# One-token shift of the values: each 127-row transfer made as one of 112 rows and one of 15 rows

## The chip, the cores and the metric

The kernel runs on one core of a Trainium2 chip. The core has a matrix engine (TensorE, PE in the profile), a vector engine (VectorE, DVE), a scalar engine (ScalarE, ACT), a general engine (GpSimd, POOL) and a sync engine (SyncE, SP), which issues nearly all DMA transfers here. Each engine works through its own instructions in order, and they wait for one another through semaphores. 16 DMA engines carry out the transfers. The metric is the device time of one execution in microseconds (us).

## The reference

One layer of a decoder trunk for 1024 tokens of width 1024, all in float32. After an RMSNorm, one projection gives q, k and v (8 heads of 64) and two inputs of a gated convolution branch. The two branches are joined, projected, added to x, and a feed-forward part of width 2816 with a short convolution follows.

```python
h = rms_norm(x, norm1_g)
q, k, v, glu_a, glu_b = split(h @ w_in)
A = stick_breaking_attention(rms_norm(q), rms_norm(k), v)
c = causal_depthwise_conv(glu_a * sigmoid(glu_b))     # 31 taps, 512 channels
C = silu(layer_norm(c))
x = x + concat([A, C]) @ w_out
gate, val = split(rms_norm(x, norm2_g) @ w_up)
x = x + (silu(causal_depthwise_conv(gate)) * val) @ w_down
```

The attention's weights are `beta[t,s] * prod_{s<j<t} (1 - beta[t,j])`, with `beta = sigmoid(q.k / 8)` and s < t. Such a weight is the difference of two neighbouring running products. So the kernel can leave the running products as they are and multiply them by differences of neighbouring values, `v[s-1] - v[s]`. For that it needs v shifted by one token.

## The kernel before, in words

Tokens lie on the 128 partitions (rows), in 8 tiles of 128 tokens. Float32 products are made in three matmuls from a high and a low part of each operand (`mm3`, lines 318 to 321): ACT copies the high part, DVE or GpSimd subtracts to get the low part. The weights of the first stage are loaded and split in this way by `weights` (load L461, high part L465, low part L469).

The heads are worked in two blocks of four. `project` makes q, k and v for a block; v of a block is `[128, 8, 256]`: row, token tile, four heads' values. The functions that matter here, in the order of the work:

- `glu` makes one of four channel blocks of the convolution. TensorE multiplies for both halves of the tokens; ACT evicts the gate (L627) and DVE the product (L629) into `cpad`. Then DVE runs 16 and 15 taps (`conv_a` L650, L652; `conv_b` L660, L662), while ACT (L669, L676) and GpSimd (L679) build the rest of the sum, which DVE joins (L692 to L694).
- `differences` (L479) shifts v of one block by one token into `ahead` (L492, L493), and GpSimd then subtracts (L501), in two halves of four token tiles. It is called for block 0 early, among the convolutions, and for block 1 when the last products of the first stage are done.
- `conv_norm` normalizes the convolution's output in two token halves: TensorE transposes (L715, L741), DVE takes statistics (L719, L720) and normalizes (L723), ACT applies the gate (L745, L768) and copies a high part (L763), DVE or GpSimd make the low part (L774), and SP stores both to device memory (`conv_d`, L785). The high and low parts lie in four rooms, the `nb` rooms, which the first convolution used before and the attention uses after; one of them already holds the first head's keys at that time.
- The attention then goes through the heads: transposes of keys (`kT`, L1054) and queries (`qT`, L1088), scores (`z`, L1131, L1132), sigmoid (L1139), a running product by a scan (L1153), its transpose (`wT`, L1180) and the product with the differences (`po`, L1208). `qk` products of the second block (`queries_keys_in`) run beside it.

After that come the output projections, the feed-forward's up products (`u`, 22 steps) and down products (`dn`, L1807).

What sets the order is a planner, `Plan`. Each operation is added with a cost for each engine that may do it, a due time (`key`) and what it must come after. `run` then chooses greedily, one operation at a time, by the earliest possible start and the due time, and `in_order` fixes the resulting order for PE, DVE, ACT and GpSimd. SP isn't fixed by it: the order of the transfers on SP is left to the framework's scheduler, which also moved other loads between the two halves of one shift. For SP the planner has a model of its own (lines 180 to 184): `kb` is the size of an operation's transfers and `dmas` their number.

```python
for _ in range(op.dmas):
    at[e] = max(at[e] + 60, landed[-8] if len(landed) > 7 else 0)
    dma = max(dma, at[e] + (2300 if start < 3000 else 1300)) + op.kb * 2.6 / op.dmas
    landed.append(dma + 600)
op.end = landed[-1]
```

Of the kernel before, what the change touches and what calls it, by code (L numbers as in the profile page):

```python
# [16 lines left out]
P = 128  # L17
# [39 lines left out]
class Plan:  # L57
# [32 lines left out]
    def add(self, cost, *args):  # L90
        if not isinstance(cost, dict):
            cost, args = {cost: args[0]}, (lambda eng, f=args[1]: f(),) + args[2:]
        op = Plan.Op()
        op.shares = "DVE2" in cost
        op.cost, op.emit, op.key = {e.rstrip("2"): c for e, c in cost.items()}, args[0], args[1]
        op.after = list(args[2]) if len(args) > 2 else []
        op.takes = list(args[3]) if len(args) > 3 else []
        op.end, op.engine, op.n, op.kb, op.dmas = None, None, len(self.ops), 512, 1
        self.ops.append(op)
        return op  # L100
# [101 lines left out]
def kernel(  # L202
# [21 lines left out]
    nc = tc.nc  # L224
    x, out = x[0], out[0]
# [128 lines left out]
    def wide(token, shape, name, dt=F32):  # L354
        if token.index < 2:
            return wp.tile(shape, dt, tag=f"raw{token.index}", name=name)
        return convp.tile(shape, dt, tag=f"co{token.index - 2}", name=name)
# [121 lines left out]
    def differences(blk, key, after, tokens):  # L479

        d = {}

        def shift():
            v = qkv["v", blk]
            if tokens:
                d["s"] = [wide(t, [P, 4, 256], f"ahead{blk}_{n}") for n, t in enumerate(tokens)]
            else:
                whole = qkvp.tile([P, NT, 512], F32, tag="qk1", name="ahead0")
                d["s"] = [whole[:, 4 * n:4 * n + 4, :256] for n in range(2)]
            nc.gpsimd.memset(d["s"][0][0:1, 0, :], 0.0)  # L490
            for n in range(2):
                nc.sync.dma_start(d["s"][n][1:P], v[0:P - 1, 4 * n:4 * n + 4, :])  # L492
                nc.sync.dma_start(d["s"][n][0:1, 1 - n:4, :], v[P - 1:P, 3 * n:3 + 4 * n, :])  # L493

        x = add("SP", 5000, shift, key, after, tokens)
        x.kb, x.dmas = 1024, 4
        subs = []
        for n in range(2):
            def sub(eng, n=n):
                v = qkv["v", blk][:, 4 * n:4 * n + 4, :]  # L500
                (nc.gpsimd if eng == "POOL" else nc.vector).tensor_tensor(v, d["s"][n], v, op=ALU.subtract)  # L501

            subs.append(add({"POOL": 2560}, sub, key, [x]))
        for t in tokens:
            t.users += subs
        done["v", blk] = subs
# [342 lines left out]
    glu(0, glu0, *ats[0])  # L849
    project("v", 0, v0, (2, 3), (46, 52))  # L850
    differences(0, T(85), done["v", 0] + norm_done, [])
    glu(1, w1, *ats[1])
    for c in (2, 3):
# [56 lines left out]
    for n, r in enumerate(rooms):  # L910
        r.only = (n,)
    differences(1, DIFF_AT, done["v", 1] + second_used, rooms)

    def make_one():
# [156 lines left out]
    for h, half in [(h, half) for h in range(H) for half in range(2)]:  # L1071
# [4 lines left out]
        qd, room, s, d = plan.token("qd"), plan.token("q"), plan.token("s"), {}  # L1076
# [22 lines left out]
        x = add("SP", 4000, double, base - 4.0, (list(qk_done.values()) if not half else []) + early["v"] if blk else done["q", 0] + conv_done, [qd])  # L1099
# [9 lines left out]
        for g in (2 * half, 2 * half + 1):  # L1109
            ws = []  # L1110
            for u in range(2):
# [9 lines left out]
                d = {}  # L1121
# [46 lines left out]
            for sp in range(g + 1):  # L1168
                diag = sp == g
                s, th, tl, d = plan.token("s"), plan.token("thd" if diag else "th"), plan.token("tld" if diag else "tl"), {}  # L1170
# [677 lines left out]
```

## Time and profile before

| | |
|---|---|
| median of 3 runs | 1165.69 us (1165.58 to 1166.18) |
| the profiled execution, whole time | 1165.78 us |
| its span in the profile | 1164.0 us |
| TensorE busy | 1114.2 us (96% of the span) |
| VectorE busy | 892.0 us (77%) |
| ScalarE busy | 640.4 us (55%) |
| GpSimd busy | 551.1 us (47%) |
| mean granted TensorE clock | 0.982 of full speed |
| shift transfers: issues of 127 rows | 4, 508 KB each |

The span is the time from the first to the last instruction that the profiler recorded, and the whole time of that execution is 1.78 us longer. Rows of a timeline give start, duration, engine, source line, operation, what is written and read, and in brackets how long the engine sat idle before it and what ended that. "SPq" rows are the issue of a transfer on SP, not the transfer itself. The granted clock is the share of full speed that TensorE was allowed; the DMA share is the mean busy share of the 16 DMA engines.

### The profile page before, as it was taken

To read this page: it belongs to the slowest core of one execution; us is meant where nothing else is said; L and a number is where in the kernel's file an instruction comes from. 1 tells how busy PE (TensorE), PEld (TensorE's weight loads), DVE (VectorE), ACT (ScalarE), POOL (GpSimd) and SP (SyncE) were. 2 spreads that over 40 slices of the span, in tenths; PEclk is the share of its full clock that TensorE was granted. 3 is DMA by queue.
4 is the path that set the end of the run, shared out by engine and by line. 5 is a ranking of instruction groups with operands and counts; after the bars stand their busy time and mean duration, and the time that the engine had idled before them with its cause. 6 is when DMAs were issued, how large, how long until landed. Compare 5 with 4: busy or idle time off the path is not lost.

```text
span 1164.0 us, 15711 instructions
## 1 busy us (share of the span) xinstructions
PE 1114.2 (96%) x5639; PEld 935.3 (80%) x5639; DVE 892.0 (77%) x1179; ACT 640.4 (55%) x1246; POOL 551.1 (47%) x478
## 2 busy tenths in 40 slices
PE   7998998957989999999999999999999999999998
PEld 6887898846878888777888888888888888888886
DVE  5395987528998888689987777777778568888895
ACT  6253599537787777465443434333333368866660
POOL 5076867327323332276433331333123169987770
PEclk8999998988999999999999999999999999999999
DMA  7112111213473411542322222222222293124303
GB/s 275 35 34 78 37 37 37 68 77 110 122 223 109 127 55 38 199 171 83 108 92 91 73 91 81 83 75 89 91 73 91 91 341 111 63 83 145 145 1 145
DMA packets 109987, 118.56 MB, mean 102 GB/s; under 512 B 20857, under 2 KB 89688, under 8 KB 109910
## 3 DMA queue, kind: packets, MB, share of 16 engines
q1 hardware_dynamic: 109766, 117.05, 30.2%
q8 instruction: 44, 0.72, 0.3%
q10 hardware_dynamic: 144, 0.52, 0.1%
q14 instruction: 33, 0.27, 0.1%
HBM read 82.95 MB, written 28.31 MB: 96 GB/s over the span
## 4 chain that ended last, share of the span: by engine, by line
PE 74%; DVE 10%; DMA 5%; ACT 4%; POOL 3%; SPq 3%; issue 2%; POOLq 0%; DVEq 0%; ACTq 0%
PE dn L1807 18%; PE u_S L320 7%; PE u_S L321 7%; PE u_S L319 7%; PE u L320 5%; PE u L321 5%; PE u L319 5%; PE po L1208 2%; SPq L493 2%; DMA ahead<-v 2%; POOL attn L679 2%; DVE conv_a L652 2%; DVE nb L1153 2%; PE wT L1180 2%; DMA conv_d<-conv_hi 1%
## 5 line engine op out<-in xcount | busy, mean ns | idle before, releaser
L1807 PE MATMUL dn<-wd,wd 128*128 128x512 f32 x768 | 181.4, 389 | 0.0
L1807 PEld LDWEIGHTS dn<-wd,wd 128*128 128x128 f32 x768 | 144.1, 188 | 30.0
L320 PE MATMUL u_S<-bT,aS 128*128 128x512 f32 x264 | 102.8, 389 | 0.0
L321 PE MATMUL u_S<-bT,aS 128*128 128x512 f32 x264 | 102.7, 389 | 0.0
L319 PE MATMUL u_S<-bT,aS 128*128 128x512 f32 x264 | 102.4, 389 | 0.0
L1810 DVE TENSOR_TENSOR c<-dn,c 128x512 f32<-128x512 f32 x120 | 81.3, 684 | 27.4 <-PE dn L1807 26.9
L315 ACT CAST aS<-rawu 128x512 fp32r<-128x512 f32 x63 | 39.0, 622 | 95.5 <-PE u_S L321 68.0
L1712 ACT CAST wd<-rawd 128x512 fp32r<-128x512 f32 x128 | 72.9, 619 | 33.3 <-DMA rawd<-in_w_down_dram 9.2
L1153 DVE TENSOR_TENSOR_SCAN nb<-nb,one 128x128 f32<-128x128 f32 (+4 forms) x64 | 85.2, 1344 | 5.5 <-ACT nb L1139 4.9
L1554 POOL TENSOR_TENSOR s<-rawu 128x512 f32<-128x512 f32 x21 | 30.5, 1451 | 99.4 <-DMA rawu<-in_w_up_dram 92.1
L1711 ACT COPY whole<-rawd 128x512 f32<-128x512 f32 x110 | 63.4, 586 | 24.1 <-DVE wd L1713 12.2
L1560 POOL TENSOR_TENSOR rawu<-rawu 128x512 f32<-128x512 f32 x21 | 29.4, 1400 | 85.1 <-DVE a L316 85.1
L1713 DVE TENSOR_TENSOR wd<-whole,wd 128x512 fp32r<-128x512 f32 x90 | 59.6, 682 | 13.0 <-ACT wd L1712 6.4
L315 ACT CAST a<-rawu 128x512 fp32r<-128x512 f32 x63 | 39.0, 621 | 53.4 <-PE u_S L321 33.8
L1656 DVE SCALAR_TENSOR_TENSOR y<-gv,cols_a,y 128x1023 f32<-128x1023 f32 (+1 forms) x44 | 59.4, 1351 | 9.3 <-ACT y L1654 9.3
L319 PE MATMUL u<-b,a 128*128 128x512 f32 x168 | 66.1, 393 | 0.0
L321 PE MATMUL u<-b,a 128*128 128x512 f32 x168 | 65.9, 392 | 0.0
L320 PE MATMUL u<-b,a 128*128 128x512 f32 x168 | 65.9, 392 | 0.0
L316 DVE TENSOR_TENSOR a<-rawu,a 128x512 fp32r<-128x512 f32 x63 | 53.4, 850 | 15.5 <-ACT a L315 15.5
L320 PEld LDWEIGHTS u_S<-bT,aS 128*128 128x128 f32 x264 | 49.5, 188 | 10.7 <-issue 0.4
L319 PEld LDWEIGHTS u_S<-bT,aS 128*128 128x128 f32 x264 | 49.6, 188 | 10.3
L321 PEld LDWEIGHTS u_S<-bT,aS 128*128 128x128 f32 x264 | 49.5, 188 | 10.3
(364 smaller groups left out, 3410.5 us busy)
## 6 DMA issues: line engine op xcount, KB each, us to landing
rawu<-in_w_up_dram SPq DMA_DIRECT2D x44, 512.0 KB
act_d<-y SPq DMA_DIRECT2D x22, 512.0 KB
rawd<-act_d SPq DMA_DIRECT2D x22, 512.0 KB
rawd<-in_w_down_dram SPq DMA_DIRECT2D x22, 512.0 KB
rawo<-in_w_out_dram SPq DMA_DIRECT2D x8, 512.0 KB
m<-conv_d SPq DMA_DIRECT2D x16, 256.0 KB
xt<-in_x_dram SPq DMA_DIRECT2D x8, 512.0 KB
x_part<-xt SPq DMA_DIRECT2D x8, 512.0 KB
```

Of the source, the lines that this page charges most:

```text
L315: nc.scalar.copy(hi, src)
L316: lo_engine.tensor_tensor(lo, src, f32(hi), op=ALU.subtract)
L319: nc.tensor.matmul(ps, a_hi, b_hi, start=first, stop=False)
L320: nc.tensor.matmul(ps, a_hi, b_lo, start=False, stop=False)
L321: nc.tensor.matmul(ps, a_lo, b_hi, start=False, stop=last)
L1153: nc.vector.tensor_tensor_scan(rev, rev, ones_of[0][:, :w], 0.0, op0=ALU.mult, op1=ALU.max)
L1656: nc.vector.scalar_tensor_tensor(y[:, j:], g[:, :S - j], par("fw", (KF - 1 - j) * NF + f), y[:, j:], op0=ALU.mult, op1=ALU.add)
L1711: nc.scalar.copy(whole, src)
L1712: nc.scalar.copy(t[:, 0], src)
L1713: lo_engine.tensor_tensor(t[:, 1], whole, f32(t[:, 0]), op=ALU.subtract)
L1807: nc.tensor.matmul(ps, a[:, tok], b, start=first and m == 0, stop=last and m == 2, skip_group_check=True)
L1810: nc.vector.tensor_tensor(sums[c][s], ps, sums[c][s], op=ALU.add)
```

## The change

In `differences`, the transfer of rows 0 to 126 of v into rows 1 to 127 of `ahead` is made in two pieces: rows 0 to 111 and rows 112 to 126. Each piece is a transfer of its own on SP. The bytes and where they go are the same. The planner is told of six transfers instead of four for each call.

```diff
             for n in range(2):
-                nc.sync.dma_start(d["s"][n][1:P], v[0:P - 1, 4 * n:4 * n + 4, :])
+                for r in (slice(0, 112), slice(112, P - 1)):
+                    nc.sync.dma_start(d["s"][n][r.start + 1:r.stop + 1], v[r, 4 * n:4 * n + 4, :])
                 nc.sync.dma_start(d["s"][n][0:1, 1 - n:4, :], v[P - 1:P, 3 * n:3 + 4 * n, :])
 
         x = add("SP", 5000, shift, key, after, tokens)
-        x.kb, x.dmas = 1024, 4
+        x.kb, x.dmas = 1024, 6
```

## The prediction

> **What bounds the kernel now.** I read the page first, then the chain of waits in order of time, then the timelines of the five engines around the two places where the chain passes through the shift, then a table of stretches. The page:
>
> ```profile
> span 1164.0 us, 15711 instructions
> PE 1114.2 (96%) x5639; PEld 935.3 (80%) x5639; DVE 892.0 (77%) x1179; ACT 640.4 (55%) x1246; POOL 551.1 (47%) x478
> PE dn L1807 18%; PE u_S L320 7%; PE u_S L321 7%; PE u_S L319 7%; PE u L320 5%; PE u L321 5%; PE u L319 5%; PE po L1208 2%; SPq L493 2%; DMA ahead<-v 2%; POOL attn L679 2%; DVE conv_a L652 2%; DVE nb L1153 2%; PE wT L1180 2%; DMA conv_d<-conv_hi 1%
> ```
>
> TensorE is busy for 1114.2 of 1164.0 us, so 49.8 us is all that it idles, and only idle time or a slow granted clock can be won. The shares by line name the shift twice: "SPq L493 2%" and "DMA ahead<-v 2%". The sync queue's timeline (start, duration, line) shows both calls of `differences`:
>
> ```profile
> 21.44 0.29 SPq L808 DMA_DIRECT2D param_rows<-in_ffn_dw_w_dram  x1
> 34.15 0.86 SPq L492 DMA_DIRECT2D ahead<-v  x1
> 35.06 18.65 SPq L493 DMA_DIRECT2D ahead<-v  x1
> 53.97 0.39 SPq L461 DMA_DIRECT2D raw_glu_b<-in_w_in_dram  x1
> 69.39 0.75 SPq L492 DMA_DIRECT2D ahead<-v  x1
> 70.19 18.60 SPq L493 DMA_DIRECT2D ahead<-v  x1
> 88.88 0.39 SPq L461 DMA_DIRECT2D raw_glu_b<-in_w_in_dram  x1
> ...
> 216.43 0.69 SPq L492 DMA_DIRECT2D ahead<-v  x1
> 217.18 8.66 SPq L493 DMA_DIRECT2D ahead<-v  x1
> ...
> 227.09 18.62 SPq L493 DMA_DIRECT2D ahead<-v  x1
> 245.76 0.58 SPq L785 DMA_DIRECT2D conv_d<-conv_hi  x1
> ```
>
> Each 127-row transfer (L492) is issued in 0.69 to 0.86 us in the rows shown, but the tiny transfer behind it (L493, 3 or 4 runs of 1 KB) holds SP for 8.66 to 18.65 us; another small one, L808, takes 0.29 us. I read that as SP waiting for room behind the big one. The stretches say how fast that runs (columns: window, its length, busy time of PE, PEld, DVE, ACT, POOL, granted clock, DMA share, GB/s):
>
> ```profile
> 72.00:88.00 16.00, 16.00 (x72) 13.27 (x71) 13.62 (x18) 4.64 (x9) 8.05 (x8) 1.00 0.07 24
> 90.00:94.00 4.00, 4.00 (x20) 3.30 (x19) 0.00 (x0) 0.00 (x0) 0.00 (x0) 1.00 0.89 256
> 183.30:190.00 6.70, 2.07 (x14) 1.67 (x13) 6.59 (x8) 6.70 (x19) 3.59 (x5) 0.81 0.00 0
> 190.00:200.00 10.00, 10.00 (x69) 10.00 (x69) 7.86 (x11) 9.56 (x45) 9.42 (x10) 0.79 0.35 107
> 262.61:270.00 7.39, 5.44 (x25) 4.68 (x26) 5.86 (x11) 4.42 (x8) 5.49 (x7) 0.54 0.33 108
> 270.00:350.00 80.00, 72.46 (x447) 61.51 (x446) 75.83 (x96) 64.08 (x120) 35.73 (x37) 0.98 0.50 155
> 350.00:500.00 150.00, 145.16 (x875) 122.98 (x874) 125.87 (x159) 104.97 (x197) 51.48 (x58) 1.00 0.33 108
> ```
>
> From 72 to 88 us, with the shift alone in flight, the share of the 16 engines is 0.07, about 1 of 16, at 24 GB/s; from 90 to 94 us two 128-row weight loads run at 0.89 and 256 GB/s. So 127 rows go through one engine. The Trainium skill (DMA: Bandwidth & Descriptors, section "Why a DMA increments its semaphore by 16 and not by 1") says that a transfer gets the largest number of engines up to 16 that divides the row counts of both sides, and names 127 rows as a case of one. By that, 112 rows get 16 engines and 15 rows get 15; the trace agrees on 127 and on 128, and shows neither 112 nor 15.
>
> Who pays, in the chain of waits:
>
> ```profile
> 70.19 25.03 DMA ahead<-v
> 245.76 15.19 DMA conv_d<-conv_hi
> ```
>
> **First call (block 0).** GpSimd, DVE and TensorE rows, with the idle time before an instruction and its releaser in brackets:
>
> ```profile
> 95.38 2.40 POOL L501 TENSOR_TENSOR v<-ahead,v 128x1024 f32<-128x1024 f32 x1 [15.08 <-DMA ahead<-v]
> 52.72 1.23 DVE L469 TENSOR_TENSOR lo_glu_b<-raw_glu_b,hi_glu_b 128x1024 fp32r<-128x1024 f32 x1 [5.65 <-ACT hi_glu_b L465]
> 98.86 0.69 DVE L692 TENSOR_TENSOR attn<-attn,conv_a 128x512 f32<-128x512 f32 x1 [12.85 <-POOL attn L679]
> 102.20 0.68 DVE L629 TENSOR_TENSOR cpad<-glu_a,cpad 128x512 f32<-128x512 f32 x1
> 90.13 0.39 PE L321 MATMUL glu_a<-h_hi,lo_glu_a 128*128 128x512 f32 x1
> 59.52 11.84 DVE L652 SCALAR_TENSOR_TENSOR conv_a<-cpad,cols_b,conv_a 128x512 f32<-128x512 f32 x15
> ```
>
> and TensorE's waits in 98 to 130 us and in 180 to 192 us (total, times, longest):
>
> ```profile
> PE glu_b L319 <- DVE cpad L629: 2.8, 3, 1.5
> PE glu_a L319 <- ACT cpad L627: 0.5, 1, 0.5
> PE v L320 <- DVE lo_v L469: 3.6, 1, 3.6
> PE v L319 <- ACT hi_v L465: 1.0, 1, 1.0
> ```
>
> The subtraction L501 stands in GpSimd's order before the last convolution sum of channel block 0, so that sum, and the DVE behind it, wait 15.08 and 12.85 us for the transfer. TensorE doesn't stop then: its glu products run on to 101.4. But it finished the input of the next channel block at 90.4 (last glu_a at 90.13, bound by PE), and the DVE takes it only at 102.20. So the DVE's tap chain, near saturation after that, runs 102.20 - 90.4 = 11.8 us late, and TensorE meets it again and again: 2.8 + 0.5 = 3.3 us before 130, then 1.0 + 3.6 = 4.6 us for the weights of v, whose low half waits its turn on the DVE. After that stop the clock is 0.79 for 10 us.
>
> **Second call (block 1).** Here TensorE stops outright:
>
> ```profile
> 235.86 0.69 DVE L774 TENSOR_TENSOR conv_lo<-conv_out,conv_hi 128x512 fp32r<-128x512 f32 x1
> 241.21 0.60 ACT L763 CAST conv_hi<-conv_out 128x512 fp32r<-128x512 f32 x1
> 261.05 0.69 DVE L774 TENSOR_TENSOR conv_lo<-conv_out,conv_hi 128x512 fp32r<-128x512 f32 x1 [19.76 <-DMA conv_d<-conv_hi]
> 265.09 0.81 DVE L723 TENSOR_SCALAR attn<-ln,mv,lr 128x512 f32<-128x512 f32 x1
> 247.47 0.39 PE L321 MATMUL qk<-hi_qk,h_lo 128*128 128x512 f32 x1
> 262.61 1.44 PE L1054 MATMUL kT<-ident_r,first_keys 128*128 128x128 f32 x8 [14.75 <-DVE attn L723]
> 266.00 1.09 PE L1088 MATMUL qT<-ident_r,attn 128*128 128x128 f32 x4 [1.95 <-issue]
> ```
>
> The first pair of conv halves is ready at 236.6 (235.86 + 0.69), but its store L785 stands on SP behind L493 until 245.76, and then takes 15.19 us because its share of the one engine queues behind the shift. The next low half (261.05) needs the room that this store reads, the DVE waits 19.76 us, and the key transposes behind it wait 14.75 us. Their second wait of 1.95 us, before qT, is the same DVE backlog (L723, 265.09 + 0.81 = 265.9).
>
> **The change part by part.**
> Removed: four transfers of 508 KB (127 x 4 x 1 KB) on one engine, and with them L493's 18.65 + 18.60 + 8.66 + 18.62 = 64.5 us on SP. Added: four more issues on SP. The nearest rows are L492's 0.69 to 0.86 us and L808's 0.29, so 1.2 to 3.4 us in total; I take 4 x 0.7 = 2.8, beside the 64.5 that go, so SP is never later than before. Two more transfers per call also mean two more completions for L501 to wait for, all in flight together: nothing, because they end with the larger one.
> New duration: at the 256 GB/s row, 448 KB lands in 1.8 us; at the 24 GB/s row, in 19 us. I take the first, since 0.07 against 0.89 is what one engine against sixteen would show. The 15 rows (60 KB) take 0.2 to 2.5 us by the same two rows; either end is hidden, the room is some 7 us (below).
> Moved: behind the first call on SP stand the weight loads L461 at 53.97 and 88.88; they can go once their rooms are free, and TensorE didn't wait for them, so nothing is gained or lost directly. Behind the second stands the conv store.
>
> The sum, by TensorE's own stops:
> A. The stop of 14.75 us goes. Store issued at 236.6, 512 KB at 256 GB/s is 2 us, say landed by 240; the high half is ready at 241.8 (241.21 + 0.60), the low half at about 242.5 instead of 261.7, and the rest of the DVE's burst (261.05 to 265.9, 4.85 us) is done by 247.3, before TensorE's last qk product at 247.47. Bounds 9.8 (if the whole 4.85 us burst ended up behind TensorE) to 14.75; I take 14.75.
> B. The 1.95 us goes with the same burst; bounds 0 to 1.95.
> C. In 262.61 to 270 the granted clock is 0.54: 5.44 us of PE at that clock is 2.5 us more than at 1.00, which TensorE has without the stop; bounds 0 to 2.5.
> D. The 3.3 us before 130 go, since the DVE is 11.8 us earlier and TensorE at most 3.3; bounds 0 to 3.3.
> E. Of the 4.6 us at 185 to 190 the DVE's own 1.23 us for a low half (L469 at 52.72) stays, so 3.4 goes; with it 10 x (1 - 0.79) = 2.1 us of slow clock. Bounds 0 to 6.7; I take 5.5, because the DVE will be 8 us or more ahead there. What is late next is ACT's high half (the wait of 1.0 us).
> Sum: 14.75 + 1.95 + 2.5 + 3.3 + 5.5 = 28.0 us.
>
> After 270 all engines start from the same backlog, only earlier, so I carry the whole shift to the end: from 350 on TensorE is the bound (145.16 of 150.00 us, and nearly all afterwards). From 270 to 350 the DVE is (75.83 of 80.00 us), but it is released 19 us earlier as well. The profiled execution took 1165.78 us, 1.78 outside the span, and the median of the runs is 1165.69, the same within 0.1. 1165.78 - 28.0 = 1137.8, rounded to **1138**.
>
> A rule speaks against it. The Trainium skill (same page, section "Rules for kernel authors") says that two transfers to disjoint parts of the partitions aren't worth making, because they serialize on the same 16 engines. By that alone the sum would be zero; the trace has the unsplit transfer on one engine's share, which that rule presupposes isn't so.
>
> **The rivals.**
> 1. Only the second call counts. The front of the kernel is bound by TensorE for 30 to 100 us, and ACT is near saturation at 183 to 190 (6.70 busy of 6.70), so D and E could be replaced by waits for ACT. Then A + B + C = 19.2, time 1146.6. For: that saturation; against: the four waits on the DVE are named. 13 in 100.
> 2. More is won: the attention's start (7.5 us of PE idle from 270 to 350) also loses stops, because DVE and ACT get their backlog done under TensorE's qk products instead of with it. Up to 5 us more, 1133 or lower. For: the burst ends before 247.47 now. Against: the DVE is 95% busy there. 8 in 100.
> 3. The order changes. The planner in the kernel is told six transfers instead of four; it counts the same end for them, but moves its SP clock by 120 ns, and its greedy choice can fall another way from there on, as can the order on SP. A changed order that meets one 15-tap half chain (the 15 taps that took 11.84 us from 59.52) costs what it adds: 1149.6, range 1147 to 1160. 8 in 100.
> 4. The pieces gain nothing: 112 rows also run on one engine. Then 448 KB at 24 GB/s is 19 us again, time 1165.8. For: no row shows 112. Against: 128 rows do spread. (The rule against splitting would end here too.) 3 in 100.
> 5. Slower: the new order hits the attention. From 270 to 500 there are 32 steps (8 heads x 2 halves x 2 groups) in which TensorE waits for scans; PE idles 7.5 + 4.8 = 12.4 us over them, 0.4 us a step. If a worse order costs 1 us more a step, 32 us are lost: 1169.8. It decides from 28.0 / 32 = 0.88 us a step. For: the DVE's 95%; against: by its lines 180 to 184 the plan reckons 4.6 us for four pieces and for six, so it already assumes a quick landing. 6 in 100.
>
> **How the numbers follow.** The likeliest case, 62 in 100, has 1138; its own range is 1132 (half of rival 2's surplus) to 1144 (E missing). Adding rival 1 and the near ends of 2 and 3 gives 1131 to 1150, which leaves out about 2 in 10. A change of 0.2% (2.3 us) is about what a measurement of this kernel can tell from none. Faster: 62 + 13 + 8 + 8 = 91; same: 3; slower: 6.
>
> **What would show it.** Right: L493 takes under 1 us each time; no stretch with the shift alone in flight at share 0.07; L501 no longer waits 15 us; TensorE's stop between the last qk product and kT is under 1 us, and the granted clock stays near 1.00 there; the DVE takes channel block 1's input within 1 us of 90.4. PE's idle total falls from 49.8 to about 26 us, the rest of the gain being clock. Wrong, and where: a second call with a short L493 but the low half still waiting for its store (A); v's weights still late, now for ACT (E); another order of the same lines on TensorE or the DVE (3, 5); L493 still long (4).

## The result, and the profile after

The changed kernel takes 1136.55 us (median) against 1165.63 us: a ratio of 0.9748, 95% interval 0.9729 to 0.9767, that is 29.1 us less. One of the four runs of the changed kernel took 1837.24 us at a granted clock of 0.556 (the others 0.992 to 0.994); the ratio leaves it out, and the median would be 1136.36 us without it. The forecast was 1138 (1131 to 1150). The profiled execution took 1136.74 us, its span is 1134.9 us. The page after:

```profile
span 1134.9 us, 15718 instructions
PE 1108.3 (98%) x5639; PEld 931.5 (82%) x5639; DVE 891.3 (79%) x1179; ACT 640.8 (56%) x1246; POOL 551.0 (49%) x478
PE 88%; DVE 7%; ACT 2%; DMA 1%; issue 1%; POOL 1%; SPq 0%; DVEq 0%; ACTq 0%; POOLq 0%
```

TensorE's idle time is 1134.9 - 1108.3 = 26.6 us, where it was 49.8 and the forecast said about 26, and its busy time fell by 5.9 us for the same 5639 instructions, with a mean granted clock of 0.992 where it was 0.982. The chain of waits now lies on PE for 88% (74% before), and SP and the shift have no part in it that the page shows.

The order of the instructions on PE, DVE, ACT and GpSimd is the same in both kernels, instruction by instruction, and on SP it is the same but for the four added transfers. So rivals 3 and 5 of the prediction fall, and whatever moved, moved because a transfer landed at another time. (Lines behind L492 have numbers higher by one after the change: L493 is now the large pieces, L494 the small transfer, L502 the subtraction.) The sync queue after:

```profile
33.97 1.81 SPq L493 DMA_DIRECT2D ahead<-v  x2
35.82 0.76 SPq L494 DMA_DIRECT2D ahead<-v  x1
...
69.22 1.64 SPq L493 DMA_DIRECT2D ahead<-v  x2
70.91 0.70 SPq L494 DMA_DIRECT2D ahead<-v  x1
...
207.88 1.42 SPq L493 DMA_DIRECT2D ahead<-v  x2
209.34 0.77 SPq L494 DMA_DIRECT2D ahead<-v  x1
...
224.01 0.36 SPq L786 DMA_DIRECT2D conv_d<-conv_hi  x1
```

The small transfer is issued in 0.70 to 0.77 us where it held SP for up to 18.65, and the store of the first high half goes out at 224.01, as soon as that half is made. The stretch behind the issue at 69.22, with the shift alone in flight:

```profile
71.00:73.00 2.00, 2.00 (x11) 1.65 (x10) 1.93 (x4) 1.65 (x3) 2.00 (x3) 1.00 0.71 203
```

The DMA share is 0.71 at 203 GB/s where 127 rows ran at 0.07 and 24 GB/s, so the 112 rows do spread; how many engines exactly isn't shown. GpSimd, DVE and PE at the two places where the prediction showed the waits:

```profile
80.09 2.40 POOL L502 TENSOR_TENSOR v<-ahead,v 128x1024 f32<-128x1024 f32 x1
90.39 0.69 DVE L630 TENSOR_TENSOR cpad<-glu_a,cpad 128x512 f32<-128x512 f32 x1 [1.21 <-PE glu_a L321]
230.00 0.69 DVE L775 TENSOR_TENSOR conv_lo<-conv_out,conv_hi 128x512 fp32r<-128x512 f32 x1 [0.55 <-ACT conv_hi L764]
234.61 0.81 DVE L724 TENSOR_SCALAR attn<-ln,mv,lr 128x512 f32<-128x512 f32 x1
235.87 0.80 PE L1055 MATMUL kT<-ident_r,first_keys 128*128 128x128 f32 x8
236.50 0.62 PE L1089 MATMUL qT<-ident_r,attn 128*128 128x128 f32 x4
```

The subtraction no longer waits (15.08 us before). The DVE takes the next channel block's input at 90.39, when TensorE has just made it (102.20 before). The low half that stood 19.76 us now waits 0.55 us, for ACT's high half, and both transposes follow the last qk product without a gap. TensorE's longest waits are now:

```profile
PE hT L438 <- DVE x_q L429: 5.0, 2, 3.8
PE z L1132 <- ACT nb L1140: 4.2, 4, 2.0
```

cpad, v's weights, kT and qT are gone from the list, and the two shown were there before (5.2 and 3.6 us). To see where the 29.1 us came from, the same instruction is looked up in both traces; of before:

```profile
101.01 0.39 PE L321 MATMUL glu_a<-h_hi,lo_glu_a 128*128 128x512 f32 x1
138.39 0.28 PE L319 MATMUL k<-hi_k,h_hi 128*128 128x256 f32 x1
214.67 0.40 PE L319 MATMUL qk<-hi_qk,h_hi 128*128 128x512 f32 x1
279.96 0.79 PE L1054 MATMUL kT<-ident_r,keys 128*128 128x128 f32 x8
335.78 0.66 PE L1088 MATMUL qT<-ident_r,attn 128*128 128x128 f32 x4 [0.17 <-ACT keys L1058]
```

and of after (the first k product, the first qk product, the second kT, a later qT):

```profile
133.71 0.28 PE L319 MATMUL k<-hi_k,h_hi 128*128 128x256 f32 x1
202.82 0.40 PE L319 MATMUL qk<-hi_qk,h_hi 128*128 128x512 f32 x1
249.85 0.80 PE L1055 MATMUL kT<-ident_r,keys 128*128 128x128 f32 x8
306.92 0.66 PE L1089 MATMUL qT<-ident_r,attn 128*128 128x128 f32 x4 [0.16 <-ACT keys L1059]
```

The lead is 4.68 us at the first k product, 11.85 at the first qk product, 262.61 - 235.87 = 26.74 at the first kT, 266.00 - 236.50 = 29.50 at qT, 30.11 at the second kT, and 28.86 at the later qT. Of this, 0.16 us were there before the first call could matter (a glu_a product at 100.10 before and 99.94 after). So the first call gave 11.7 us, the second 18.3, and the attention's start took 1.2 back.

### The profile page after: what moved, and what is told of

Read it like the earlier page. It is cut to its first block, busy times and chain, and to the rows that moved or that the text cites. A ratio compares the mean times of both kernels' runs of the same rounds, so it can differ in the third digit from the quotient of the medians.

```text
span 1134.9 us, 15718 instructions
## 1 busy us (share of the span) xinstructions
PE 1108.3 (98%) x5639; PEld 931.5 (82%) x5639; DVE 891.3 (79%) x1179; ACT 640.8 (56%) x1246; POOL 551.0 (49%) x478
## 4 chain that ended last, share of the span: by engine, by line
PE 88%; DVE 7%; ACT 2%; DMA 1%; issue 1%; POOL 1%; SPq 0%; DVEq 0%; ACTq 0%; POOLq 0%
PE dn L1808 18%; PE u_S L320 7%; PE u_S L321 7%; PE u_S L319 7%; PE u L321 5%; PE u L319 5%; PE u L320 5%; PE po L1209 2%; DVE nb L1154 2%; PE wT L1181 2%; PE v L321 1%; PE v L320 1%; PE v L319 1%; PE glu_b L319 1%; PE glu_b L321 1%; PE glu_a L319 1%
```

## The experiments

The theory: the number of rows decides how many DMA engines carry a piece, and the time of large pieces on one engine is the cost, once it is more than a call has room for. Against it stand: that two smaller pieces help as such; that the hold on SP is the cost; that only one of the two calls counts. In every kernel below the order on PE and DVE is that of the kernels above; on ACT and GpSimd too, except that ACT also issues the stores in the last.

**Each call by itself.** The split is made in one of the two calls of `differences` (an edit of the kernel before; the planner is still told of four transfers):

```diff
-                nc.sync.dma_start(d["s"][n][1:P], v[0:P - 1, 4 * n:4 * n + 4, :])
+                for r in (slice(0, 112), slice(112, P - 1)) if blk == 0 else (slice(0, P - 1),):
+                    nc.sync.dma_start(d["s"][n][r.start + 1:r.stop + 1], v[r, 4 * n:4 * n + 4, :])
```

> Only the call for block 0 is split (112 + 15 rows); the call for block 1 keeps its 127 rows. In the profile of the changed kernel the first qk product of the first stage comes 11.85 us earlier than before (202.82 against 214.67). Theory (the two calls' gains add): 1165.6 - 11.9 = 1153.8 us, and the 14.7 us stop before the key transposes is still there. Rival (what the first call wins is swallowed by the second call's stop): 1165.6 us.

Measured 1154.67 us (ratio 0.991, 0.9894 to 0.9927). With `blk == 1` instead:

> Only the call for block 1 is split; the call for block 0 keeps its 127 rows. Theory (the gains add): of the 29.1 us, 29.1 - 11.85 = 17.2 us belong to this call, so 1148.4 us, with the waits of TensorE for cpad (3.3 us) and v's weights (4.6 us) as before. Rival (only this call counts, the front is hidden): 1136.6 us.

Measured 1146.65 us (0.9841, 0.9826 to 0.9856). Among TensorE's longest waits, first of the kernel that splits only the first call, and then of the one that splits only the second:

```profile
PE kT L1055 <- DVE attn L724: 15.6, 1, 15.6
```

```profile
PE v L320 <- DVE lo_v L469: 3.6, 1, 3.6
PE glu_b L319 <- DVE cpad L630: 2.8, 3, 1.6
PE z L1132 <- ACT nb L1140: 4.2, 4, 2.0
```

Each split removes the waits of its own call and leaves the other's. The gains are 11.0 and 19.0 us, 30.0 together against 29.1 for both: they add, to within 1 us. Both one-call rivals fall, the prediction's rival 1 among them.

**Pieces that don't spread.** Still two pieces in both calls, of 113 and 14 rows:

```diff
-                for r in (slice(0, 112), slice(112, P - 1)):
+                for r in (slice(0, 113), slice(113, P - 1)):
```

> Two pieces again in both calls, but of 113 and 14 rows. Theory (the row count decides how many DMA engines carry a piece; 113 has no divisor up to 16 but 1): the large piece still goes through one engine, 452 KB at 24 GB/s is 18.9 us instead of 21.2, so 2.3 us are won in the first call and 4.7 us in the second, 1158.6 us, and the small transfer holds the sync queue as before. Rival (that there are two pieces is what helps): 1136.6 us.

Measured 1159.04 us (0.9945, 0.993 to 0.996). SP, TensorE and a stretch with the shift alone in flight in that kernel:

```profile
68.38 17.17 SPq L493 DMA_DIRECT2D ahead<-v  x2
221.75 16.94 SPq L493 DMA_DIRECT2D ahead<-v  x2
PE kT L1055 <- DVE attn L724: 10.6, 1, 10.6
70.00:84.00 14.00, 14.00 (x64) 11.58 (x63) 13.64 (x18) 4.53 (x8) 9.03 (x8) 1.00 0.07 22
```

One row moved from the smaller piece to the larger costs 22.5 us. So not the number of pieces but the row count does it: 112 rows spread, 113 don't: their DMA share is 0.07 again. This bears out what the Trainium skill says (DMA: Bandwidth & Descriptors, "Why a DMA increments its semaphore by 16 and not by 1"), for 113 as well as for 127. My expectation was wrong in one detail: the small transfer no longer holds SP. The hold is now in L493, whose second issue waits behind its first.

**How much room there is.** Pieces of 66 and 61 rows, and of 97 and 30; 61 and 97 have no divisor up to 16 but 1:

```diff
-                for r in (slice(0, 112), slice(112, P - 1)):
+                for r in (slice(0, 66), slice(66, P - 1)):     # and: slice(0, 97), slice(97, P - 1)
```

> Two pieces of 66 and 61 rows in both calls; 61 rows (244 KB) should go through one engine in 10.2 us. Theory (the shift costs nothing until it is later than its room): it lands about 83 us in the first call, where the subtraction wants it at 80.1 and the next channel block is not taken before 90.4, and in the second call two of them end about 226, where the store is wanted landed at 230; so 1136.6 us, within 0.3%. Rival (time on the one engine costs in proportion to its bytes): 1136.6 + 29 x 61 / 127 = 1150.5 us.

Measured 1136.87 us (0.9754, 0.974 to 0.9769).

> Two pieces of 97 and 30 rows in both calls; 97 rows (388 KB) through one engine take 16.2 us. Theory (only what is later than its room costs): in the first call the subtraction is released near 89 instead of 80, and the next channel block is taken some 5 us late instead of 11.8; in the second call two such pieces end near 237.5, the store lands near 238.5 and the key transposes come some 4 to 6 us late: about 1147 us, between 1143 and 1152. Rival (cost in proportion to the bytes on the one engine): 1136.6 + 29 x 97 / 127 = 1158.7 us.

Measured 1152.49 us (0.9886, 0.9871 to 0.9901), outside both numbers. The kernel of 66 and 61 rows first, GpSimd and DVE:

```profile
85.18 2.41 POOL L502 TENSOR_TENSOR v<-ahead,v 128x1024 f32<-128x1024 f32 x1 [5.40 <-DMA ahead<-v]
231.03 1.78 DVE L775 TENSOR_TENSOR conv_lo<-conv_out,conv_hi 128x512 fp32r<-128x512 f32 x1 [2.00 <-DMA conv_d<-conv_hi]
```

and the kernel of 97 and 30 rows, with DVE, and TensorE's waits:

```profile
96.31 0.68 DVE L630 TENSOR_TENSOR cpad<-glu_a,cpad 128x512 f32<-128x512 f32 x1
246.26 0.69 DVE L775 TENSOR_TENSOR conv_lo<-conv_out,conv_hi 128x512 fp32r<-128x512 f32 x1 [10.93 <-DMA conv_d<-conv_hi]
PE kT L1055 <- DVE attn L724: 5.9, 1, 5.9
PE v L320 <- DVE lo_v L469: 3.6, 1, 3.6
PE qT L1089 <- issue: 1.9, 1, 1.9
```

| rows on one engine | time, us | us per row, to the line above |
|---|---|---|
| none (112 + 15) | 1136.55 | |
| 61 | 1136.87 | 0.005 |
| 97 | 1152.49 | 0.43 |
| 113 | 1159.04 | 0.41 |
| 127 | 1165.63 | 0.47 |

The theory was right that there is room, and that it isn't in proportion: the first 61 rows are free, with the waits just appearing (5.40 us at the subtraction, 2.00 at the low half). Above that each row costs 0.41 to 0.47 us. That is near an estimate from the 24 GB/s of the trace before: a row is 4 KB, so 0.17 us; the first call delays the DVE by one transfer, the second the store by two, 0.5 us in all. My 1147 for 97 rows was too low: the stop for v's weights stayed whole (3.62 us), and I had left out the 1.9 us at qT and the slow clock behind the stop.

**More of the spread shift.** Both pieces made twice:

```diff
-                for r in (slice(0, 112), slice(112, P - 1)):
+                for r in 2 * (slice(0, 112), slice(112, P - 1)):
```

> Both pieces (112 and 15 rows) are made twice, so the shift's bytes and issues double, still spread. Theory (the spread shift has room to spare in both calls): 1136.6 us, within 0.2%. Rival (the issues or the bytes of the spread shift are on the path now): about 3 us an issue pair more in each half, so 1139 us or more.

Measured 1135.34 us (0.9742, 0.9726 to 0.9758): twice the bytes and issues cost nothing. The spread shift is off the path with room to spare, so there is no more to win from this transfer.

**The hold on SP, or the engine behind it.** The single 127-row transfers are kept. First, the small transfers are issued before the large ones:

```diff
             for n in range(2):
-                nc.sync.dma_start(d["s"][n][1:P], v[0:P - 1, 4 * n:4 * n + 4, :])
                 nc.sync.dma_start(d["s"][n][0:1, 1 - n:4, :], v[P - 1:P, 3 * n:3 + 4 * n, :])
+            for n in range(2):
+                nc.sync.dma_start(d["s"][n][1:P], v[0:P - 1, 4 * n:4 * n + 4, :])
```

> The shift keeps its single 127-row transfers; in each pair the small transfer is issued before the large one, so that the first large one of each call no longer has a small one waiting directly behind it. Theory (the time of the large transfers on the one engine is the cost, and the hold on the sync queue only its sign): whatever is issued next is held instead and the store lands as late, 1165.6 us, within 0.3%; at most 2 us less, since the small transfer no longer ends last. Rival (the hold of the small transfers on the sync queue is the cost): 1145 us or less.

Measured 1163.28 us (0.9984, 0.9975 to 0.9993). SP, DVE and TensorE there:

```profile
34.46 0.78 SPq L494 DMA_DIRECT2D ahead<-v  x1
76.57 12.21 SPq L461 DMA_DIRECT2D raw_glu_b<-in_w_in_dram  x1
232.42 10.21 SPq L786 DMA_DIRECT2D conv_d<-conv_hi  x1
258.28 0.69 DVE L775 TENSOR_TENSOR conv_lo<-conv_out,conv_hi 128x512 fp32r<-128x512 f32 x1 [20.43 <-DMA conv_d<-conv_hi]
PE kT L1055 <- DVE attn L724: 15.4, 1, 15.4
```

The transfers of the first call no longer hold SP, yet only 2.0 us are won against the 1165.24 us of before in the same comparison: the hold has moved to what is issued next, a weight load (12.21 us) and the store itself (10.21 us), and the low half waits 20.43 us. So the place of the hold isn't the cost. The gain begins in the first call: its first subtraction starts at 79.69 instead of 95.38, because the small transfer whose landing it waited for (issued at 70.19 and landed 25.03 us later in the chain of before) no longer stands behind the large one. This run can't show what a kernel without any hold would take.

Second, only the stores of conv_d change their queue:

```diff
-                        nc.sync.dma_start(conv_d[n][:, j, c - 1:c + 1, :], f32(d[part, c // 2]))
+                        nc.scalar.dma_start(conv_d[n][:, j, c - 1:c + 1, :], f32(d[part, c // 2]))
```

> The shift keeps its single 127-row transfers as before; only the stores of conv_d are issued by ScalarE on its own DMA queue instead of by SyncE. They no longer stand behind the shift on the sync queue, but share the same DMA engine with it. Theory A (what delays the store is its place behind the shift in one queue; two queues take turns on the engine): the second call's stop goes, about the time of the kernel that splits only the second call, 1146.7 us, up to 3 us more because ScalarE waits for the low half before it issues. Theory B (the one engine works off the shift first, whichever queue asks): about 1164 us.

Measured 1150.9 us (0.9876, 0.9861 to 0.9891). ACT's and SP's queues, a stretch, DVE and PE:

```profile
236.26 0.33 ACTq L785 DMA_DIRECT2D conv_d<-conv_hi  x1
227.50 22.29 SPq L493 DMA_DIRECT2D ahead<-v  x1
240.00:244.00 4.00, 4.00 (x20) 3.27 (x19) 2.59 (x6) 3.56 (x11) 2.75 (x6) 1.00 0.07 28
242.96 0.69 DVE L774 TENSOR_TENSOR conv_lo<-conv_out,conv_hi 128x512 fp32r<-128x512 f32 x1 [1.27 <-DMA conv_d<-conv_hi]
248.11 0.80 PE L1054 MATMUL kT<-ident_r,first_keys 128*128 128x128 f32 x8
PE z L1131 <- ACT nb L1139: 8.6, 6, 3.5
```

Theory A holds, though the time is 1.2 us above what it allowed. The store goes out at 236.26 and the low half starts at 242.96 instead of 261.05, although the shift still has its engine busy (share 0.07 from 240 to 244) and SP is held even longer (22.29 us); TensorE's 14.75 us stop is gone. So what delayed the store was its place behind the shift in one queue, and a second queue gets its turns on the same engine. The time is 4.2 us above the kernel that splits only the second call, and the trace names one place for it: the scores wait longer for ACT (8.6 us; 4.2 in the second experiment), which now also issues the stores.

## Why the prediction was right, step by step

- *One engine for 127 rows, many for 112 and 15:* shown for 127 and 112 by the DMA shares (0.07 and 0.71) and by the step from 112 to 113 rows; the 15 rows alone aren't shown. The Trainium skill's rule that the prediction set against itself (DMA: Bandwidth & Descriptors, "Rules for kernel authors": two transfers to disjoint partition halves aren't worth making) doesn't hold for this transfer, because the unsplit one doesn't spread. Rival 4 falls.
- *A, 14.75 us:* 26.74 - 11.85 = 14.89 measured. The path was right too: the DVE's burst ends at 234.61 + 0.81 = 235.42, before the transposes start at 235.87; the forecast's 247.3 less 11.85 is 235.45.
- *B and C, 1.95 + 2.5 us:* the lead grows from 26.74 at the first kT to 29.50 at qT and 30.78 at a qk product a little later (270.10 before, 239.32 after), 4.0 us in all, 0.4 less than the two terms. With B's 1.95 us of standing still in it, the clock gave 2.1 us and not 2.5. C was likely too large because I took the mean clock of a stretch that held those 1.95 us, and charged it to the busy time alone.
- *D, 3.3 us:* 4.68 - 0.16 = 4.5 measured, above the bound I had set. I summed the idle column, and a stop costs more than it shows. Before, the last matmul ahead of the first stop started at 101.01, so by the 0.23 us pitch the next was due at 101.24; it came at 102.94, 1.70 us late, with 1.54 in the idle column, which counts from the modelled end of the matmul. The one behind it came after 0.33 us (103.27) instead of 0.23. Four such stops make some 1.0 of the missing 1.2 us.

```profile
102.94 0.50 PE L319 MATMUL glu_b<-h_hi,hi_glu_b 128*128 128x512 f32 x1 [1.54 <-DVE cpad L629]
```

- *E, 5.5 us:* 11.85 - 4.68 = 7.17 measured, above its bound of 6.7. The first v product behind the stop came 189.63 - 179.90 = 9.73 us earlier, so 5.05 us are the stops and 2.1 the clock. I kept 1.23 us for the DVE's own low half, but it was ready when TensorE came; the other 0.4 us are what the idle column hides, as under D. The clock part was right: the v products run at 1.00 now, where the 4 us after the stop had 0.50 and the whole slice 0.79.

```profile
190.00:194.00 4.00, 4.00 (x20) 4.00 (x20) 3.89 (x6) 3.78 (x19) 3.84 (x4) 0.50 0.74 225
190.00:200.00 10.00, 10.00 (x86) 10.00 (x85) 4.89 (x6) 7.31 (x17) 6.19 (x5) 1.00 0.29 75
```

(The first row is of before, the second of after.)

- *Carried to the end:* nearly. The lead falls from 30.78 at 270 to 28.86 at 336. Some 0.7 us go at a score that waits for ACT (0.88 us at 248.06 after, 0.23 at 278.17 before). The other 1.2 us are clock, of which the prediction had nothing here: the same qk products ran at 1.00 before and at 0.50 after. Why the clock stayed low for longer after the change is open. Rival 2, that the attention's start would win more, went the other way.

```profile
290.00:292.00 2.00, 2.00 (x10) 1.55 (x10) 2.00 (x3) 1.91 (x4) 1.13 (x3) 1.00 0.30 69
260.00:262.00 2.00, 2.00 (x6) 1.52 (x6) 2.00 (x3) 1.79 (x4) 1.15 (x2) 0.50 0.36 82
```

(Again before, then after.)

- *Two slips in the working:* the lower bound of A is 14.75 - 4.85 = 9.9, not 9.8, and half of rival 2's 5 us would put the low end of the likeliest case at 1135.3, not 1132. Neither moves the forecast.

So the mechanism was right in both calls, but D and E came out 2.9 us larger than forecast, and B, C and the way to the end 2.3 us smaller. That the sum, 28.0 against 29.1, came closer than its terms is luck.

## What to carry to other kernels

When a small transfer holds its queue for many microseconds, look at the transfer ahead of it and at the DMA share while it runs: a share near 1 of 16 was one engine here, and a row count without a divisor up to 16 other than 1 was the reason. Splitting such a transfer into pieces with good row counts pays only where something waits; the cost of the bad one is found not at its own reader alone, but at whatever stands behind it in the same queue, here a store that had nothing to do with it. Work that must not wait behind a slow transfer can also go to another queue.

## What the runs showed of the hardware that I had not expected

The step from 112 to 113 rows was expected from the row counts once the experiments began, but it is sharp: 22.5 us for one row, with the same bytes. A second queue got its turns here even on an engine that had a long list of work from the first: 6.7 us passed from the store's issue (236.26) to the start of the work that waited for it (242.96), beside 15.19 us from issue to landing on the shared queue.
